# Spatial weights of the gating unit: loaded and masked between the halves of the v projection, transposed right behind the row statistics

## The chip, the cores and the metric

The kernel runs on one core of a Trainium2 chip, as one launch. The metric is the device time of one execution in microseconds (us); the time of a kernel is the median of its runs. Engines are named as in the profile: PE (TensorE matmul), PEld (its weight load), DVE (VectorE), ACT (ScalarE), POOL (GpSimd), SP (SyncE, which issues nearly all DMAs here).

## What is computed

Two blocks follow one another on a sequence of 1024 rows of width 1024, all in float32. The first block has two layers (`DEPTH = 2`), and only these are touched by the change. A layer normalizes and modulates its input, multiplies it with `w_in`, and splits the product into u, v, z_a (512 columns each) and the parts of a sparse attention (q, k, val, z_b, and an indexer q_idx, k_idx, w_idx that picks 256 keys for each row). The gating unit is

```
vn = layer_norm(v, g_v, b_v).reshape(bn, s // CHUNK, CHUNK, A_GROUPS, A_GDIM)
w_m = jnp.where(causal[None], w_s, jnp.zeros_like(w_s))
mixed = jnp.einsum('gts,bcsgd->bctgd', w_m, vn) + b_s.T[:, :, None]
return u * mixed.reshape(bn, s, A_WIDTH)
```

so `w_spatial` (8 groups of 128x128) must be masked to its lower triangle and stand on the chip transposed before it can multiply the normalized v. Then silu(z_a) times this, next to the gated attention, goes through `w_out`, and a layer norm ends the layer. The second block (windowed attention, convolution, a mixture of 32 experts) takes the other half of the time and is not changed.

## The kernel before

The 1024 rows are 8 tiles of 128 partitions. A float32 product is made of three matmuls on split operands (`mm3`, lines 100 to 102): hi x hi, hi x lo, lo x hi. `dense_nat` is one projection of 256 columns: 8 k-steps, 8 row tiles, three matmuls each, into two tiles of PSUM ("big"); it takes its weights from `wnext`, which loads 128x512 (`wraw`, L136), rounds it on ACT (`whi`, L108) and subtracts on POOL (`wlo`, L111). In a layer the projections come in the order narrow columns, q_idx (two halves, six tiles), v (two halves, evacuated into X[:, :, 0] by `ev_c`, L781), u (two halves, into X[:, :, 1]), q (two halves), z_a, z_b.

Work that isn't projection is spread among the matmuls in two ways. Generators in the list `bgs` are stepped by `bg`, which `dense_nat` calls 16 times with 650 units each (10,400 a projection; 487.5 and 7,800 where six tiles are projected); a generator yields the units that a step costs, and the list is worked off in order. `flush(bgs)` behind the u projection runs what is left. In `streams` run the two selections of keys (`select`, tiles 2, 4, 6 and 3, 5, 7): transposes of q_idx (`heads_T`, L538, evacuated to `qT` by L543 and L544), score matmuls (L628), relu on ACT into `rel` (L631), weighted sums on DVE (L634, L636), then a search of many short DVE instructions (L606 to L686).

In `bgs` stand first `ada_late` (three parts in layer 0, one in layer 1; a part has two halves, a half has four loads of `adaw`, eight DVE products of 650 units, L463 and L465, and three more steps, 8,300 units in all), then `sgu`, the gating unit. `sgu` loads the norm's rows `vg`, loads `ws` and masks it on POOL (L795), loads the bias `bs`, takes the statistics of eight tiles (L802, L803; 700 units each), makes `rsv` (L84) and `nbv` (L808), normalizes each tile on ACT (L811) and multiplies and adds `vg` on POOL (L812, L813; 1,400 units each), transposes `ws` by `to_T` (PE L504 into two PSUM banks "tr", ACT L506 into `wmh`, DVE L507 into `wml`; 1,300 units), and then for each of eight groups splits v into `vs` (ACT L108, POOL L111), multiplies by `wmh` and `wml` on PE and applies u and the bias on DVE (L830).

`adaw`, `vg`, `ws`, `wmh`, `wml` and `vs` share one ring of four buffers, the tag "w4"; the two banks "tr" also serve `heads_T`; `rel`, `code`, `pl` and the accumulators of `ada_late` share six buffers, the tag "r2". The kernel is first traced in the order of the Python code; a scheduler then gives each engine its own fixed order, by readiness in a model of time and, among ready instructions, by the order of tracing. So a load stands in SP's queue where its buffer came free, not where the code has it.

Of the kernel before, what the change touches and what calls it, by code (L numbers as in the profile page):

```python
# [26 lines left out]
NT = 8  # L27
# [13 lines left out]
def tile_hybrid(ctx, tc, I, out):  # L41
# [18 lines left out]
    def bank(shape, kind):  # L60
        if kind in banks["turn"]:
            n = banks["turn"][kind] % banks[kind]
            banks["turn"][kind] += 1
            if n < 2:
                return psum2.tile(shape, FT, name=kind)
            return banks["pool"].tile(shape, FT, name=kind + "x", bufs=banks[kind] - 2)
        return banks["pool"].tile(shape, FT, name=kind, bufs=banks[kind])
# [13 lines left out]
    def rsqrt(dst, var, eps, n):  # L81
        t = small.tile([128, 16], FT, name="rsq")
        V.tensor_scalar(t[:, :n], var, eps, None, op0=OP.add)
        G.tensor_tensor(dst, t[:, :n], mhalf[:, :n], op=OP.pow)  # L84
# [14 lines left out]
    def mm3(o, lh, ll, rh, rl, start, stop):  # L99
        T.matmul(o, lh, rh, start=start, stop=False, skip_group_check=True)  # L100
        T.matmul(o, lh, rl, start=False, stop=False, skip_group_check=True)  # L101
        T.matmul(o, ll, rh, start=False, stop=stop, skip_group_check=True)  # L102

    def split(hi, lo, src, which="pool", sub=None):
        if which == "pool":
            G.tensor_scalar(hi, src, 1.0, 0.0, op0=OP.mult, op1=OP.add)
        elif which == "act":
            A.activation(hi, src, AF.Copy)  # L108
        else:
            V.tensor_copy(hi, src)  # L110
        return (sub or V).tensor_tensor(lo, src, hi.bitcast(FT), op=OP.subtract)  # L111
# [37 lines left out]
    def wnext():  # L149
        if not ready:  # L150
            ready.append(wstage(*plan.pop(0)))
        r = ready.pop(0)
        if plan and plan[0] is None:
            plan.pop(0)
        elif plan:
            ready.append(wstage(*plan.pop(0)))
        return r
# [44 lines left out]
    def bg(budget, ns=None):  # L202
        due[0] += budget
        while bgs and due[0] > 0:
            due[0] -= step(bgs)
        if not bgs:
            due[0] = 0.0
        now[0] += budget * 2.0 if ns is None else ns
        while True:
            ready = [x for x in streams if not x[2] or now[0] >= x[1] + MARGIN]  # L210
            if not ready:
                break
            s_ = min(ready, key=lambda x: x[1])
            if max(dve[0], s_[1]) > now[0] + AH:
                break
            resume(s_)
# [10 lines left out]
    def dense_nat(n, KT, lhs, tiles, evac, bgt=1300.0):  # L227
        nb = (len(tiles) + 3) // 4
        ps = [bank([128, 4, 256], "big") for _ in range(nb)]
        for k0 in range(0, KT, 2):  # L230
            hi, lo = wnext()
            for b in range(nb):
                for kk in range(2):
                    k = k0 + kk
                    for i in range(4 * b, min(4 * b + 4, len(tiles))):
                        t = tiles[i]
                        mm3(ps[b][:, i % 4, :n], lhs(k, 0, t), lhs(k, 1, t), hi[:, kk, :n], lo[:, kk, :n],
                            start=(k == 0 and i % 2 == 0), stop=(k == KT - 1))
                    if k + 1 == KT:
                        for i in range(4 * b, min(4 * b + 4, len(tiles)), 2):  # L240
                            evac(tiles[i], ps[b][:, i % 4:i % 4 + 2, :n])
                    bg(bgt * len(tiles) / 8 / nb, 3 * min(4, len(tiles) - 4 * b) * n / 2.4)
# [35 lines left out]
    def load_row(dst, src, n):  # L278
        nc.sync.dma_start(dst, rows_of(src, n))
# [220 lines left out]
    def to_T(src, t, hi, lo, n, half=None):  # L500
        for b in range(n // 4) if half is None else (half,):
            ps = bank([128, 4, 128], "tr")
            for j in range(4):
                T.transpose(ps[:, j, :], src[:, (b * 4 + j) * 128:(b * 4 + j + 1) * 128], ident)  # L504
            d = (slice(None), slice(b * 4, b * 4 + 4), slice(t * 128, (t + 1) * 128))
            A.activation(hi[d], ps, AF.Copy)  # L506
            V.tensor_tensor(lo[d], ps, hi[d].bitcast(FT), op=OP.subtract)  # L507
# [51 lines left out]
    def layer(l, xin, hT=None):  # L559
# [4 lines left out]
        lhs = lambda k, a, t: hT[a][:, k, t * 128:(t + 1) * 128]  # L564
# [214 lines left out]
        def ev_c(sl, c, scale=1.0):  # L779
            def f(t, ps):  # L780
                A.activation(X[:, t:t + 2, sl, c * 256:(c + 1) * 256], ps, AF.Copy, scale=scale)  # L781
            return f
        for c in range(2):
            dense_nat(256, 8, lhs, range(NT), ev_c(0, c))

        def sgu():
            vg = tmp.tile([128, 2, 512], FT, name="vg", tag="w4", bufs=4)
            load_row(vg[:, 0, :], I["v_norm_g"][l], 512)
            load_row(vg[:, 1, :], I["v_norm_b"][l], 512)

            wmh = tmp.tile([128, 8, 128], FR, name="wmh", tag="w4", bufs=4)
            wml = tmp.tile([128, 8, 128], FR, name="wml", tag="w4", bufs=4)
            ws = tmp.tile([128, 8, 128], FT, name="ws", tag="w4", bufs=4)
            nc.sync.dma_start(ws, I["w_spatial"][l].rearrange("g t s -> t g s"))
            G.affine_select(ws, ws, pattern=[[0, 8], [-1, 128]], compare_op=OP.is_ge, fill=0.0, base=0,  # L795
                            channel_multiplier=1)
            bs = small1.tile([128, 8], FT, name="bs", bufs=1)
            nc.sync.dma_start(bs, I["b_spatial"][l].rearrange("g t -> t g"), allow_slow_non_contiguous=True)
            mvs = small1.tile([128, NT, 2], FT, name="mvs", bufs=1)
            for t in range(NT):  # L800
                st = small1.tile([128, 6], FT, name="bst1")
                V.bn_stats(st, X[:, t, 0, :])  # L802
                V.bn_aggr(mvs[:, t, :], st)  # L803
                yield 700.0, 650.0
            rsv = small1.tile([128, NT], FT, name="rsv", bufs=1)
            rsqrt(rsv, mvs[:, :, 1], 1e-5, NT)
            nbv = small1.tile([128, NT], FT, name="nbv", bufs=1)
            V.scalar_tensor_tensor(nbv, mvs[:, :, 0], -1.0, rsv, op0=OP.mult, op1=OP.mult)  # L808
            for t in range(NT):
                xv = X[:, t, 0, :]  # L810
                A.activation(xv, xv, AF.Identity, scale=rsv[:, t:t + 1], bias=nbv[:, t:t + 1])  # L811
                G.tensor_tensor(xv, xv, vg[:, 0, :], op=OP.mult)  # L812
                G.tensor_tensor(xv, xv, vg[:, 1, :], op=OP.add)  # L813
                yield SG1
            to_T(ws.rearrange("p g s -> p (g s)"), 0, wmh, wml, 8)
            yield 1300.0, 1200.0
            vss = {}
            for g in range(9):
                if g < 8:
                    vs = vss[g] = tmp.tile([128, 2, NT, 64], FR, name="vs", tag="w4", bufs=4)  # L820
                    split(vs[:, 0], vs[:, 1], X[:, :, 0, g * 64:(g + 1) * 64], "act", G)
                    yield SG2
                if g == 0:
                    continue
                g -= 1
                vs = vss.pop(g)
                ps = bank([128, NT, 64], "sm")
                mm3(ps, wmh[:, g, :], wml[:, g, :], vs[:, 0], vs[:, 1], True, True)
                xu = X[:, :, 1, g * 64:(g + 1) * 64]
                V.scalar_tensor_tensor(xu, ps, bs[:, g:g + 1], xu, op0=OP.add, op1=OP.mult)  # L830
                yield SG3, 660.0
# [298 lines left out]
    lhs = lambda k, a, t: hT[a][:, k, t * 128:(t + 1) * 128]  # L1130
# [486 lines left out]
    def gather(tcol, b):  # L1617
        return G.indirect_dma_start(out=XG[b][0:SL], out_offset=None, in_=h2d,
                             in_offset=bass.IndirectOffsetOnAxis(ap=tcol, axis=0), bounds_check=S - 1, oob_is_err=False)

    def split_e(raw):
        w_ = mo.tile([128, 2, 8 * 256], FR, name="ew", bufs=3)
        for h in range(2):
            c = slice(h * 1024, (h + 1) * 1024)
            split(w_[:, 0, c], w_[:, 1, c], raw[:, c], "act", V)
        return w_
# [55 lines left out]
    for e in range(NXG - 1):  # L1682
        g = gather(ti[:, e:e + 1], e)
# [3 lines left out]
    xTs, hid, ws, wds = {0: prep(0)}, {}, {}, {}  # L1687
# [47 lines left out]
    with tc.For_i(0, nov, 1) as b:  # L1735
# [14 lines left out]
        ws = [split_e(r) for r in raw]  # L1750
# [38 lines left out]
```

## Time and profile before

| | |
|---|---|
| median of 3 runs | 2372.64 us (2372.11 to 2374.22) |
| the profiled execution | 2371.94 us, span of the trace 2369.8 us |
| PE busy, PEld busy | 2140.5 us (90%), 1883.9 us (79%) |
| DVE, ACT, POOL busy | 1521.2, 1082.8, 1082.0 us |
| layer 0, layer 1, second block begin at about | 60, 700, 1310 us |

The profile is one execution. Its own time is 2.1 us above the span and 0.7 us under the median. A wait of an engine is named by what released it. The granted TensorE clock is a share of 2.4 GHz.

### The profile page before, as it was taken

The numbers are of one execution on the slowest core, as the hardware profiler recorded it, in microseconds if no ns is written. First come the engines' busy times: TensorE is split into PE (matmuls) and PEld (weight loads), VectorE is DVE, ScalarE is ACT, GpSimd is POOL, SyncE is SP. The second block draws the span as 40 slices with busy tenths as digits, with TensorE's granted clock in tenths as the row PEclk, the third lists the DMA queues.
The fourth block names the chain that finished last, engine by engine and source line by source line (L and its number), as shares of the span: only waits on it lengthen the run. The fifth ranks groups of instructions, "written<-read, shape, count | busy, mean of one in ns | idle before, by whom it ended". The sixth has DMA issues, their size and how long they took to land. (4 is left out here: it accounts for less than half of the span.)

```text
span 2369.8 us, 35974 instructions
## 1 busy us (share of the span) xinstructions
PE 2140.5 (90%) x13235; PEld 1883.9 (79%) x13235; DVE 1521.2 (64%) x3191; ACT 1082.8 (46%) x1943; POOL 1082.0 (46%) x1018
## 2 busy tenths in 40 slices
PE   5998998798989979997998999999999797999896
PEld 4898897587879979876887888888888586888785
DVE  9768887677753769685776348861010345888784
ACT  4333443554642443436554335652121222778774
POOL 4664575556736553845554345532244412222221
PEclk9999998899999989998999999999999998999998
DMA  7522112312114111223111111122121256999994
GB/s 239 188 79 86 53 32 81 106 59 68 41 47 138 45 36 49 66 67 108 68 45 41 44 41 34 30 52 67 49 67 45 98 209 200 311 325 326 317 329 116
DMA packets 146392, 260.88 MB, mean 110 GB/s; under 512 B 24681, under 2 KB 101889, under 8 KB 133905
## 3 DMA queue, kind: packets, MB, share of 16 engines
q1 hardware_dynamic: 139024, 241.59, 31.1%
q0 software_dynamic: 7168, 16.79, 3.2%
q8 instruction: 105, 1.72, 0.3%
q14 instruction: 95, 0.77, 0.1%
HBM read 228.83 MB, written 37.90 MB: 113 GB/s over the span
## 5 line engine op out<-in xcount | busy, mean ns | idle before, releaser
L111 POOL TENSOR_TENSOR wlo<-wraw,whi 128x512 fp32r<-128x512 f32 (+1 forms) x188 | 249.8, 1329 | 484.9 <-ACT whi L108 459.2
L101 PE MATMUL big<-wlo,s 128*128 128x256 f32 (+1 forms) x1536 | 440.4, 288 | 16.0 <-POOL wlo L111 16.0
L100 PE MATMUL big<-whi,s 128*128 128x256 f32 (+1 forms) x1536 | 437.8, 289 | 13.6 <-ACT s L506 8.4
L102 PE MATMUL big<-whi,s 128*128 128x256 f32 (+1 forms) x1536 | 439.6, 288 | 0.0
L101 PEld LDWEIGHTS big<-wlo,s 128*128 128x128 f32 x1536 | 301.2, 196 | 22.8 <-POOL wlo L111 19.6
L100 PEld LDWEIGHTS big<-whi,s 128*128 128x128 f32 x1536 | 298.6, 196 | 21.9 <-ACT s L506 11.0
L102 PEld LDWEIGHTS big<-whi,s 128*128 128x128 f32 x1536 | 300.6, 196 | 3.1 <-issue 0.9
L108 ACT ACTIVATE whi<-wraw 128x512 fp32r<-128x512 f32 (+1 forms) x188 | 117.7, 627 | 385.2 <-PE big L102 127.2
L111 DVE TENSOR_TENSOR ew<-s,ew 128x1024 fp32r<-128x1024 f32 x138 | 162.8, 1220 | 39.0 <-ACT ew L108 37.9
L636 DVE SCALAR_TENSOR_TENSOR s<-rel,widx,s 128x384 f32<-128x384 f32 (+3 forms) x140 | 130.6, 957 | 85.1 <-ACT rel L631 83.6
L100 PE MATMUL sm<-ew,xT 128*96 128x256 f32 x512 | 147.6, 288 | 4.8 <-ACT xT L1636 4.8
L108 ACT ACTIVATE ew<-s 128x1024 fp32r<-128x1024 f32 x138 | 137.7, 1050 | 28.6 <-PE sm L102 18.8
L102 PE MATMUL sm<-ew,xT 128*96 128x256 f32 x512 | 148.6, 290 | 1.3 <-DVE xT L1637 1.2
L101 PE MATMUL sm<-ew,xT 128*96 128x256 f32 x512 | 146.3, 286 | 0.9 <-DVE ew L111 0.9
L631 ACT ACTIVATE rel<-sm 128x384 f32<-128x384 f32 (+3 forms) x160 | 80.5, 522 | 124.1 <-PE sm L628 114.7
L100 PE MATMUL half<-s,whi 128*128 128x512 f32 x320 | 130.7, 408 | 7.1 <-ACT s L953 3.1
L101 PE MATMUL half<-s,whi 128*128 128x512 f32 x320 | 128.7, 402 | 0.0
L102 PE MATMUL half<-s,wlo 128*128 128x512 f32 x320 | 127.3, 401 | 0.0
L1674 POOL DMA_INDIRECT out_dram<-yt,ti x32 | 58.2, 1820 | 136.0 <-DMA out_dram<-yt,ti 61.0
L606 DVE TENSOR_SCALAR_CACHE_REDUCE bias<-code,cand 128x512 bf16<-128x512 int16 (+5 forms) x126 | 114.1, 924 | 0.5
L878 POOL TENSOR_SCALAR Z<-Z,rc 128x128 f32<-128x128 f32 (+7 forms) x88 | 63.9, 738 | 83.3 <-DVE rc L876 50.7
L100 PE MATMUL big<-s,whi 128*128 128x512 f32 x256 | 99.7, 390 | 0.3 <-DVE convf L1335 0.3
(618 smaller groups left out, 6014.3 us busy)
## 6 DMA issues: line engine op xcount, KB each, us to landing
wraw<-in_w_in_dram SPq DMA_DIRECT2D x164, 256.0 KB, 2.8
adaw<-in_w_ada_dram SPq DMA_DIRECT2D x48, 512.0 KB, 4.5
s<-in_w_gate_e_dram SPq DMA_DIRECT2D x23, 1024.0 KB, 9.2
s<-in_w_up_e_dram SPq DMA_DIRECT2D x23, 1024.0 KB, 11.0
s<-in_w_down_e_dram SPq DMA_DIRECT2D x23, 1024.0 KB, 11.3
X<-in_w_gate_e_dram SPq DMA_DIRECT2D x9, 1024.0 KB, 10.1
X<-in_w_up_e_dram SPq DMA_DIRECT2D x9, 1024.0 KB, 9.8
X<-in_w_down_e_dram SPq DMA_DIRECT2D x9, 1024.0 KB
```

Source lines behind the costliest of these rows:

```text
L100: T.matmul(o, lh, rh, start=start, stop=False, skip_group_check=True)
L101: T.matmul(o, lh, rl, start=False, stop=False, skip_group_check=True)
L102: T.matmul(o, ll, rh, start=False, stop=stop, skip_group_check=True)
L108: A.activation(hi, src, AF.Copy)
L111: return (sub or V).tensor_tensor(lo, src, hi.bitcast(FT), op=OP.subtract)
L606: V.tensor_scalar(junk[:, :src.shape[1]], src, thr, 0.0, op0=op, op1=OP.add, accum_out=cnt)
L631: A.activation(rel[:, :w_], ps[:, :w_], AF.Relu, scale=0.125)
L636: V.scalar_tensor_tensor(d, rel[:, :w_], widx[:, i, h:h + 1], d, op0=OP.mult, op1=OP.add)
L878: G.tensor_scalar(P[hh][:, :n], P[hh][:, :n], rc[:, hh:hh + 1], 1.0, op0=OP.mult, op1=OP.mult)
L1674: return G.indirect_dma_start(out=out, out_offset=bass.IndirectOffsetOnAxis(ap=ycol, axis=0), in_=yt, in_offset=None, bounds_check=S - 1, ...
```

## The change

The loads of `vg`, `ws` and `bs` and the mask of `ws` move out of `sgu` into a function `sgu_in`, which is called once between the two halves of the v projection instead of behind them, so it is traced ahead of those steps of `ada_late` that are still to come. The transposes of `ws` with their evacuations (`to_T`) move from behind the eight normalizations to a place between `rsv` and `nbv`. No instruction is added or removed, and no unit of `bg` changes.

```
-        for c in range(2):
-            dense_nat(256, 8, lhs, range(NT), ev_c(0, c))
-
-        def sgu():
+        def sgu_in():
             vg = tmp.tile([128, 2, 512], FT, name="vg", tag="w4", bufs=4)
...
+            return vg, ws, wmh, wml, bs
+
+        gin = []
+        for c in range(2):
+            if c:
+                gin.append(sgu_in())
+            dense_nat(256, 8, lhs, range(NT), ev_c(0, c))
+
+        def sgu():
+            vg, ws, wmh, wml, bs = gin[0]
             mvs = small1.tile([128, NT, 2], FT, name="mvs", bufs=1)
...
             rsqrt(rsv, mvs[:, :, 1], 1e-5, NT)
+            to_T(ws.rearrange("p g s -> p (g s)"), 0, wmh, wml, 8)
+            yield 1300.0, 1200.0
             nbv = small1.tile([128, NT], FT, name="nbv", bufs=1)
...
                 yield SG1
-            to_T(ws.rearrange("p g s -> p (g s)"), 0, wmh, wml, 8)
-            yield 1300.0, 1200.0
             vss = {}
```

## Rows read from the trace of the kernel before

**Rows 1.** The page: busy time and its share of the span, and busy tenths in 40 slices.

```profile
PE 2140.5 (90%) x13235; PEld 1883.9 (79%) x13235; DVE 1521.2 (64%) x3191; ACT 1082.8 (46%) x1943; POOL 1082.0 (46%) x1018
...
PE   5998998798989979997998999999999797999896
```

**Rows 2.** Waits of PE, first those of 60 to 700 us, then those of 700 to 1280 us: who waited for whom, us in total, times, longest.

```profile
PE tr L504 <- POOL ws L795: 4.0, 1, 4.0
...
PE tr L538 <- DVE wml L507: 9.0, 1, 9.0
```

**Rows 3.** The timeline of layer 0 about that wait, PE: start, us, instruction, and in brackets the idle time before it and its releaser.

```profile
230.28 0.39 PE L100 MATMUL big<-whi,s 128*128 128x256 f32 x1 [0.98 <-ACT X L781]
234.69 0.47 PE L504 MATMUL tr<-ident,ws 128*128 128x128 f32 x1 [4.02 <-POOL ws L795]
```

**Rows 4.** The timeline of POOL in layer 0.

```profile
220.55 11.24 POOL L812 TENSOR_TENSOR X<-X,vg 128x512 f32<-128x512 f32 x8 [3.83 <-DMA vg<-in_v_norm_g_dram]
231.75 1.58 POOL L813 TENSOR_TENSOR X<-X,vg 128x512 f32<-128x512 f32 x1
233.28 1.35 POOL L795 TENSOR_SCALAR_AFFINE_SELECT ws<-ws 128x1024 f32<-128x1024 f32 x1
```

**Rows 5.** The timeline of SP's queue, in layer 0 and then in layer 1.

```profile
105.43 2.88 SPq L458 DMA_DIRECT2D adaw<-in_w_ada_dram  x2
...
164.38 3.04 SPq L458 DMA_DIRECT2D adaw<-in_w_ada_dram  x2
...
215.60 0.35 SPq L279 DMA_DIRECT2D vg<-in_v_norm_g_dram  x1
...
217.30 0.38 SPq L794 DMA_DIRECT2D ws<-in_w_spatial_dram  x1
...
731.72 0.34 SPq L279 DMA_DIRECT2D vg<-in_v_norm_g_dram  x1
...
733.75 0.83 SPq L794 DMA_DIRECT2D ws<-in_w_spatial_dram  x1
```

**Rows 6.** Busy time in stretches: the stretch and its length, then PE, PEld, DVE, ACT, POOL (instructions), the granted clock, DMA share, GB/s.

```profile
230.70:234.70 4.00, 0.01 (x1) 0.01 (x1) 2.98 (x2) 0.24 (x1) 4.00 (x4) 0.94 0.00 0
234.70:239.60 4.90, 4.90 (x26) 4.71 (x27) 2.97 (x4) 2.94 (x6) 4.90 (x4) 0.70 0.04 5
...
186.00:214.00 28.00, 24.98 (x184) 24.48 (x183) 27.84 (x95) 10.12 (x16) 5.37 (x5) 0.88 0.28 77
...
810.00:830.00 20.00, 20.00 (x168) 20.00 (x167) 19.71 (x77) 8.77 (x15) 7.75 (x6) 1.00 0.13 34
830.00:850.00 20.00, 7.02 (x31) 5.22 (x30) 19.97 (x45) 5.67 (x11) 20.00 (x16) 0.71 0.17 52
850.00:855.20 5.20, 5.20 (x24) 5.20 (x24) 5.13 (x12) 1.39 (x3) 1.21 (x1) 0.50 0.00 0
```

**Rows 7.** The timeline of layer 1, PE.

```profile
841.41 2.26 PE L538 MATMUL tr<-ident,Z 128*128 128x128 f32 x8 [8.97 <-DVE wml L507]
843.32 2.82 PE L628 MATMUL sm<-kist,qT 128*128 128x384 f32 x8
849.32 0.90 PE L628 MATMUL sm<-kist,qT 128*128 128x320 f32 x2 [3.18 <-ACT rel L631]
850.02 0.41 PE L101 MATMUL big<-wlo,s 128*128 128x256 f32 x1
```

**Rows 8.** The timeline of layer 1: two lines of DVE's own listing and one of ACT's, then two of POOL's.

```profile
841.82 0.67 DVE L507 TENSOR_TENSOR wml<-tr,wmh 128x512 fp32r<-128x512 f32 x1
...
847.51 1.22 DVE L634 TENSOR_SCALAR s<-rel,widx 128x384 f32<-128x384 f32 x1
...
848.83 0.44 ACT L631 ACTIVATE rel<-sm 128x320 f32<-128x320 f32 x1 [3.36 <-DVE s L634]
...
834.40 5.68 POOL L812 TENSOR_TENSOR X<-X,vg 128x512 f32<-128x512 f32 x4
...
841.71 2.49 POOL L111 TENSOR_TENSOR wlo<-wraw,whi 128x512 fp32r<-128x512 f32 x2
```

**Rows 9.** DVE by line and shape: count, busy us, mean ns of one. First two of 186 to 212 us (layer 0), then the same two and one more of 834 to 850 us (layer 1).

```profile
L683 DVE SCALAR_TENSOR_TENSOR bias<-s,lcand,bias 128x512 bf16<-128x512 f32 x1 | 0.7, 745 | 0.0
...
L670 DVE SCALAR_TENSOR_TENSOR s<-bias,s 128x384 f32<-128x384 bf16 x1 | 0.6, 550 | 0.0
...
L683 DVE SCALAR_TENSOR_TENSOR bias<-s,lcand,bias 128x512 bf16<-128x512 f32 x1 | 1.7, 1746 | 0.0
L670 DVE SCALAR_TENSOR_TENSOR s<-bias,s 128x384 f32<-128x384 bf16 x1 | 1.6, 1624 | 0.0
...
L606 DVE TENSOR_SCALAR_CACHE_REDUCE bias<-code,cand 128x384 bf16<-128x384 int16 x1 | 0.6, 589 | 0.0
```

**Rows 10.** The instructions on the tile `adaw` in 60 to 240 us: how long DVE sat idle for its loads (us, times), and a load's time to landing.

```profile
  DMA adaw<-in_w_ada_dram: 0.3, 1
...
DMA to landing us min/median/max: 3.9/4.4/5.2
```

**Rows 11.** The waits of PE for the split groups of v in layer 0 (timeline of PE).

```profile
275.58 0.51 PE L100 MATMUL sm<-vs,wmh 128*128 128x512 f32 x1 [1.44 <-ACT vs L108]
276.94 0.50 PE L101 MATMUL sm<-vs,wmh 128*128 128x512 f32 x1 [0.85 <-POOL vs L111]
278.44 0.67 PE L101 MATMUL sm<-vs,wmh 128*128 128x512 f32 x1 [0.55 <-POOL vs L111]
```

## The prediction

> **What bounds the kernel now.** The page comes first: PE is busy for 90% of the span and below eight tenths in 7 of its 40 slices [rows 1]. PE's order is fixed, so what can be won is a stretch in which PE stands still, and each must be read where it lies. The waits of PE by releaser, over the two layers, name the two that the change is about: 4.0 us in layer 0 for the mask of `ws`, and 9.0 us in layer 1 for `wml`, the low half of the transposed weights [rows 2]. The timelines say what stands behind each.
>
> Layer 0: PE has done its work at 230.7 and begins the transposes at 234.69 [rows 3]. It waited for POOL, and POOL was late by its queue: the mask stood behind eight multiplications with `vg` and one addition, and the first of these had itself waited until 220.55 for the load of `vg` [rows 4]. SP shows why: `vg` and `ws` were issued at 215.60 and 217.30, after the last `adaw`, because the w4 buffers were held by `adaw` until then [rows 5]. POOL had little to do before, 5.37 of 28 us in 186 to 214 [rows 6], so all of this is a matter of buffers.
>
> Layer 1: there `vg` and `ws` were issued at 731.72 and 733.75, a hundred us ahead of their use [rows 5]. What made PE wait was a bank "tr": `wml` was written late by DVE, at 841.82 for the second half, and only then the transposes of q_idx could start, at 841.41 for the first bank [rows 7, 8]. But DVE was busy for 19.71 and 19.97 of 20 us in the stretches around it [rows 6]; it was late with everything.
>
> **The change, part by part.** The terms are taken against the profiled execution, 2371.94 us, which is 0.7 under the median of 2372.64; the 0.7 is put back at the end.
>
> *Loads and mask in layer 0.* When `sgu_in` is traced, the list has worked off 7,800 + 7,800 + 10,400 = 26,000 units, three halves of `ada_late` (24,900) and two products of the fourth, so 13 of 24 `adaw` are ahead of `vg` and `ws` and 11 behind. The sixteenth `adaw` was issued by 108 us, the seventeenth at 164 [rows 5]. I expect `vg` and `ws` to take the places of the fourteenth to sixteenth, at some 100 to 110 us, at the latest those of 164 to 173. The mask is one instruction of 1.35 us on POOL [rows 4], then long over when the transposes come. So the 4.02 us of waiting [rows 3] go. After it PE ran for 4.90 us at a granted clock of 0.70 [rows 6], part of it on the lower level of 1.2 GHz; at full clock that work is 0.70 x 4.90 = 3.4 us, so 1.5 go too. Sum: -5.5 us.
>
> What is late next there? DVE was waiting itself in that stretch (busy 2.98 of 4.00), ACT too (0.24) [rows 6]. POOL was not: 4.00 of 4.00, and it would be the next bound if the multiplications stayed where they are. They don't: with `vg` on the chip they can follow the normalizations directly and lie in the 28 us in which POOL had 22.6 free. Sixteen of them at 11.24 / 8 = 1.4 us [rows 4] are 22.5 us, which just fits. So the early `vg` is the half that matters.
>
> *The 11 loads of `adaw` that now come behind.* `vg`, `wmh` and `wml` hold three of the four buffers until the additions are done, so a half of `ada_late` loads its four tiles through one or two buffers and each load of 4.4 us [rows 10] may show on DVE. Before, DVE idled for these loads once, 0.3 us [rows 10]. Below, the bound is nothing, for nobody near waits for the modulation rows; above I take 0.3 for each of the eleven, 3.3 us (all eleven in full, 48 us, would need DVE to have nothing else to do between them). I take nothing, because DVE had 2.98 of 4.00 where the first half of them would end up. On SP the later `adaw` may stand ahead of a `wraw`, whose buffers are three; covered as long as one split is ready ahead.
>
> *The mask on POOL at 100 to 120 us* adds 1.35 us there and takes it away later; 0 to +1.35, taken 0. The load of `bs` does not depend on its place in the code. In layer 1 the list had only 16,600 units of `ada_late`, so `vg`, `ws` and the mask stay where they were: 0.
>
> *The transposes ahead of `nbv`.* The eight transposes, two evacuations on ACT and two on DVE are the same instructions at the same price, 11,200 units earlier. ACT takes `wmh` ahead of the eight normalizations, which come later by two evacuations; behind them stand POOL's multiplications, not PE. In layer 1 the bank is then free when PE wants it, and the 8.97 us go from that place. What is late next is DVE: PE's next wait, 3.18 us at 849.32, is for `rel`, which ACT could write only after DVE's L634 at 847.51 had taken an older one [rows 7, 8]. In front of that L634 DVE had at most 0.3 us of gaps in 37 us [rows 6], and moving `wml` forward within a full queue does not shorten it. The transposes and scores that PE did from 841.41 to 846 would be done earlier and PE would then stand until the same 849. So layer 1 is taken at 0, with bounds from 0 to -(8.97 + 3.18) and another 0.50 x 5.2 = 2.6 of lower clock (granted clock 0.50 in the 5.2 us behind) [rows 6], -14.8.
>
> *The split groups of v in layer 0* (1.44 + 0.85 + 0.55 = 2.8 us) [rows 11] wait through a pair of `vs` buffers, which stay a pair; the earlier additions let the first pair start earlier, not the third group. Taken 0, bound -2.8.
>
> Sum: 2371.94 - 5.5 = 2366.4, with 0.7 **2367.1**. Its own range runs from 2364.3 (rows 11 too) to 2371.8 (mask and `adaw` at their upper bounds, +4.7).
>
> **The rivals.** *Layer 1's wait goes as well.* The order on the engines is made anew, and if the scores' L634 come ahead of the search's tail on DVE, or big matmuls ahead of the scores on PE, the whole -14.8 is won: 2352.3. For it: the wait is booked on exactly the bank that the change frees. Against it: DVE full at 19.97 of 20.
>
> *Nothing is won.* `vg` and `ws` get no buffer before 210 us because `adaw` keep all four, or the wait of 4 us moves to a `wlo` that now stands behind a multiplication on POOL. Then 2372.6. For the second: in layer 1 two `wlo` came at 841.71, behind 5.68 us of multiplications and one addition [rows 8]. Against the first: the trace order puts `vg` and `ws` ahead of eleven loads.
>
> *Slower: layer 0 becomes like layer 1.* With `vg` early, POOL's 22.5 us of multiplications move from beside the scores into 187 to 212 us, beside the search's tail of tiles 2 and 3, which in layer 0 was undisturbed. In layer 1 they already lie so, and there the two-input instructions of the tail are long: L683 1746 ns for 745, L670 1624 for 550, while the one-input count L606 stays at 589 [rows 9]. Eight such instructions (L670, L679, L683, L685 for two tiles) at about +1.0 make DVE 8 us later in a stretch in which it had 27.84 of 28 us [rows 6], and the first scores of tiles 4 and 5 queue behind it. If this costs PE in layer 0 all that the same neighbourhood goes with in layer 1, 8.97 + 3.18 + 2.6 = 14.8 us, the net is +9.3: 2381.9. It is slower by what can be told from the point at which PE loses more than 5.5 + 4.7 = 10.2 us. Against it: in layer 0 the scores begin at 218, some 30 us behind the first multiplication instead of 7, and products of `ada_late`, now held back by buffers, leave DVE room just there. The Trainium skill (SBUF — State Buffer, section "Who interferes with whom") states the mechanism as a rule: a DVE instruction with two SBUF inputs and a GpSimd instruction that reads SBUF share a port pair, and one that comes second waits for the whole other instruction. The trace agrees by the pairs above, 745 to 1746 ns beside 1.4 us multiplications; the rule speaks against this move, which the two waits of PE alone would not tell.
>
> **How the numbers follow.** A measurement of this kernel can tell about 0.2%, 4.7 us, from no change: 2367.9 and 2377.4 are the borders. Forecast 0.45, of which 0.30 under 2367.9 and 0.15 above; layer 1 too 0.13; nothing 0.15; slower 0.27. So faster 0.43, same 0.30, slower 0.27. The range reaches to the rivals on both sides, which are single prices with a spread of their own, 2352 to 2382: about half of each rival's outcomes at the ends, 2 in 10 together, lie outside.
>
> **What would show it.** Right: `vg` and `ws` issued ahead of 175 us in layer 0, multiplications of POOL from about 188, no wait of PE for `ws`, POOL with room from 220 on; in layer 1 the transposes at some 825 us, PE still standing before 849 with `rel` as releaser and DVE full. Wrong: a wait of PE for `wlo` or `rel` in 190 to 235 us of layer 0 (the slower rival, with L683 and L670 of layer 0 above 1.5 us); a stretch 830 to 850 with PE well above 7.02 us (the first rival); or loads still at 215. The forecast also fails where the new order moves waits in q, z_a or the attention behind, which no row here prices: they are made from the same queues by another order.

## The result, and the profile after

The changed kernel takes 2390.94 us (median of 4 runs, 2385.96 to 2394.9) against 2372.38 us of the kernel before beside it (4 runs): a ratio of 1.0073, 95% interval 1.0055 to 1.0092, some 18.5 us slower. The profiled execution, the fastest of the four, took 2385.96 us with a span of 2384.0, 14.2 more than that of before. Lines of code below the edit have new numbers: the mask is L792, the normalizations L820, the multiplications and additions with `vg` L821 and L822, the attention's lines 7 higher.

PE is as busy as before, and its dips lie elsewhere: the fourth slice (179 to 238 us) is now a 6, to be held against [rows 1].

```profile
PE 2140.5 (90%) x13235; PEld 1880.6 (79%) x13235; DVE 1521.5 (64%) x3191; ACT 1085.2 (46%) x1943; POOL 1074.0 (45%) x1018
...
PE   5996998798989979987999899999999797999996
```

The loads are where they were expected, ahead of eleven `adaw`, of which the last come at 216 us and later (SP's queue, layer 0; compare [rows 5]).

```profile
102.25 0.35 SPq L279 DMA_DIRECT2D vg<-in_v_norm_g_dram  x1
...
104.74 0.38 SPq L791 DMA_DIRECT2D ws<-in_w_spatial_dram  x1
107.26 0.37 SPq L458 DMA_DIRECT2D adaw<-in_w_ada_dram  x1
...
164.34 3.04 SPq L458 DMA_DIRECT2D adaw<-in_w_ada_dram  x2
...
191.51 0.37 SPq L458 DMA_DIRECT2D adaw<-in_w_ada_dram  x1
...
215.97 0.39 SPq L458 DMA_DIRECT2D adaw<-in_w_ada_dram  x1
...
217.56 4.91 SPq L458 DMA_DIRECT2D adaw<-in_w_ada_dram  x4
```

POOL's timeline in layer 0 shows what the early `vg` released. Eleven multiplications and additions stand ahead of the first `wlo`.

```profile
187.98 2.56 POOL L821 TENSOR_TENSOR X<-X,vg 128x512 f32<-128x512 f32 x2 [1.87 <-ACT X L820]
...
195.41 5.38 POOL L821 TENSOR_TENSOR X<-X,vg 128x512 f32<-128x512 f32 x4
200.74 1.71 POOL L822 TENSOR_TENSOR X<-X,vg 128x512 f32<-128x512 f32 x1
202.41 3.26 POOL L111 TENSOR_TENSOR wlo<-wraw,whi 128x512 fp32r<-128x512 f32 x2
205.63 7.05 POOL L822 TENSOR_TENSOR X<-X,vg 128x512 f32<-128x512 f32 x5
```

On PE the wait for the mask [rows 3] is gone: four of the transposes run at 172 us and four at 190.88, without one (the mask was made at 111 us). Two larger waits stand in its place, one for that `wlo`, one for a product of `ada_late`.

```profile
190.88 0.60 PE L504 MATMUL tr<-ident,ws 128*128 128x128 f32 x4
...
204.18 0.58 PE L101 MATMUL big<-wlo,s 128*128 128x256 f32 x1 [10.26 <-POOL wlo L111]
...
221.61 1.87 PE L469 MATMUL sm<-ada,onesf 128*1 128x512 f32 x2 [8.52 <-DVE ada L465]
```

DVE by line in 195 to 221 us (count, busy us, mean ns of one, idle time before) answers to [rows 9]; most pairs here are one instruction of 512 columns and one of 384. L670 and L683, two-input instructions of the search's tail, are now as long in layer 0 as in layer 1. `L695` works on 8 columns and takes 973 ns in the mean: the first three of the four run beside POOL's work with `vg`, 1.13 us the first and 2.47 for the next two together, and the fourth, behind POOL's last addition, takes 0.21.

```profile
L465 DVE SCALAR_TENSOR_TENSOR ada<-adaw,cb,ada 128x512 f32<-128x512 f32 x7 | 5.2, 745 | 0.5 <-DMA adaw<-in_w_ada_dram 0.5
L695 DVE SCALAR_TENSOR_TENSOR e<-rank,K,m 128x8 f32<-128x8 f32 x4 | 3.8, 973 | 0.0
L670 DVE SCALAR_TENSOR_TENSOR s<-bias,s 128x512 f32<-128x512 bf16 (+1 forms) x2 | 3.4, 1684 | 0.0
L683 DVE SCALAR_TENSOR_TENSOR bias<-s,lcand,bias 128x512 bf16<-128x512 f32 (+1 forms) x2 | 3.4, 1680 | 0.0
L679 DVE SCALAR_TENSOR_TENSOR pl<-s,lcand,place 128x512 f16<-128x512 f32 (+1 forms) x2 | 2.4, 1206 | 0.0
...
L606 DVE TENSOR_SCALAR_CACHE_REDUCE bias<-code,cand 128x384 bf16<-128x384 int16 (+1 forms) x3 | 2.0, 653 | 0.0
L463 DVE TENSOR_SCALAR ada<-adaw,cb 128x512 f32<-128x512 f32 x1 | 1.5, 1515 | 0.0
```

In layer 1 the two waits of [rows 7] are still there, 11.9 us for 12.2: what is saved on `wml` is waited for `rel`.

```profile
853.62 2.17 PE L538 MATMUL tr<-ident,Z 128*128 128x128 f32 x8 [5.79 <-DVE wml L507]
...
864.74 0.90 PE L628 MATMUL sm<-kist,qT 128*128 128x320 f32 x2 [6.07 <-ACT rel L631]
```

**Where the time went.** To place a loss, each ACT and DVE instruction of one trace is matched with the same one of before (same text of the line, same tiles, the n-th of its kind), and the median of the differences in start is taken over a stretch. The table gives the delay added (+) or made up (-) in each stretch in us, the stretches in the time of before: up to 185; from there to 515 (layer 0's gating, scores, projections); to 700 (layer 0's attention and output); to 1000 (layer 1 up to its attention); to 1160 (layer 1's attention); to 2190 (the rest). Behind 2190 us the changed kernel makes up 3.5 again, which gives the 14.2 of the spans. An entry moves by up to 1.5 us with the place at which a stretch is cut. The runs below the first are the experiments.

```
run                start  to 515  to 700  to 1000  to 1160  to 2190   sum
changed kernel      -0.1    +5.3    +9.2     +0.7     +4.0     -1.4  17.7
e1_loads_only       +0.1    +5.5    +9.6     +0.1     +0.8     +1.6  17.7
e2_transposes_only  +3.5    +0.7     0.0     -2.4    +11.8     +0.3  13.9
e3_vg_late          +1.2    -6.5    +4.4     -2.5    +15.1     -2.7   9.0
e4_layer1_only      +3.7    -2.3    -0.1     -2.8    +12.8     -3.1   8.2
n1_short_mults      -0.1   -12.8    +8.0     -0.6     +6.4     +2.7   3.6
e5_ws_layer0        +0.5    -5.8    +4.3     -1.1     +6.3     -0.6   3.6
c1_stats_number     -0.4    -2.5    -0.4     +0.3     +6.9     -1.0   2.9
c2_rope_number      +2.6    -2.4    +7.6     +0.5     +4.5     +1.2  14.0
v1_ws0_z1250        +3.3    -4.5    +1.4     -1.1     +2.6     -1.3   0.4
v2_layer1_s1000     +2.3    +1.1    +0.1     +0.9     +1.7     +3.2   9.3
v3_both_late_vg     -0.1    -2.6    +1.9     +1.0     +1.0     +1.6   2.8
v4_after_r3500      +0.3    +2.5     0.0     -0.1     +8.0     -1.8   8.9
q1_wlo_ahead        +2.4    +3.6    +8.1     +0.5     +6.1     +0.9  21.6
```

Single executions differ by themselves. Four runs have layer 0 in the order of before (e2, e4, c1, v2): they lie between -0.4 and +3.7 us in the first column and between -2.5 and +1.1 in the second. v2 is built in the order of before on every engine from start to end, as far as the traces tell, and its row is the plainest measure of this spread: its traced execution, 2379.89 us, is 9.3 behind, its median of 2374.71 is level with before. The traced execution of c1 is the fastest of its eight (2372.18 for a median of 2379.94). So a row shows where time went; what a kernel costs is told by its median. The attentions repeat better: in the third column the five runs that draw layer 0's attention in the order of before (those four and v4) stay within 0.4, and runs with one and the same other order agree (changed kernel and e1: 9.2 and 9.6; e3 and e5: 4.4 and 4.3). The changed kernel loses 5.3 ahead of layer 0's attention, 9.2 in it, and 4.0 in layer 1's: more than half of the loss of this execution lies in stretches whose code the change doesn't touch.

### The profile page after: what moved, and what is told of

The parts are those of the page before. It is cut to its first block, busy times and chain, and to the rows that moved or that the text cites. A ratio compares the mean times of both kernels' runs of the same rounds, so it can differ in the third digit from the quotient of the medians.

```text
span 2384.0 us, 35978 instructions
## 1 busy us (share of the span) xinstructions
PE 2140.5 (90%) x13235; PEld 1880.6 (79%) x13235; DVE 1521.5 (64%) x3191; ACT 1085.2 (46%) x1943; POOL 1074.0 (45%) x1018
## 5 line engine op out<-in xcount | busy, mean ns | idle before, releaser
L636 DVE SCALAR_TENSOR_TENSOR s<-rel,widx,s 128x384 f32<-128x384 f32 (+3 forms) x140 | 121.6, 891 | 87.9 <-ACT rel L631 86.4
L606 DVE TENSOR_SCALAR_CACHE_REDUCE bias<-code,cand 128x512 bf16<-128x512 int16 (+5 forms) x126 | 113.7, 924 | 0.3
L1681 POOL DMA_INDIRECT out_dram<-yt,ti x32 | 50.1, 1565 | 133.7 <-DMA out_dram<-yt,ti 76.0
```

Source lines behind the costliest of these rows:

```text
L606: V.tensor_scalar(junk[:, :src.shape[1]], src, thr, 0.0, op0=op, op1=OP.add, accum_out=cnt)
L636: V.scalar_tensor_tensor(d, rel[:, :w_], widx[:, i, h:h + 1], d, op0=OP.mult, op1=OP.add)
L1681: return G.indirect_dma_start(out=out, out_offset=bass.IndirectOffsetOnAxis(ap=ycol, axis=0), in_=yt, in_offset=None, bounds_check=S - 1, ...
```

## The experiments

The theories were: A, the multiplications with `vg`, done early, are the direct loss; B, the earlier transposes are; C, the build makes the order of the engines anew for any edit, and an attention drawn anew costs by itself; D, `adaw` is starved of buffers; E, a gain ahead of an attention turns into waits in it. Each run stands with its median, that of the kernel before beside it, and the ratio with its 95% interval.

**e1_loads_only.** The changed kernel with the transposes put back:

```
-            to_T(ws.rearrange("p g s -> p (g s)"), 0, wmh, wml, 8)
-            yield 1300.0, 1200.0
             nbv = small1.tile([128, NT], FT, name="nbv", bufs=1)
...
                 yield SG1
+            to_T(ws.rearrange("p g s -> p (g s)"), 0, wmh, wml, 8)
+            yield 1300.0, 1200.0
```

> The changed kernel with its transposes put back behind the normalizations: the loads and the mask stay early, in both layers. Theory A (the early load of vg releases POOL's sixteen multiplications and additions into the search's tail of layer 0; the big matmul's wlo stands behind them, 10.3 us, and DVE's two-input instructions lengthen): the whole loss stays, 2386 to 2394, with a wait of PE for wlo of about 10 us at 194 to 204 us. Theory B (the transposes ahead of nbv are what costs, for ACT's and DVE's evacuations come ahead of the normalizations): 2367 to 2373, without that wait. Theory C (any redrawn order of the later stages can lose ten us): no fixed time, but the first 220 us like the changed kernel's and another loss behind them than its 8 us.

Measured: 2388.45 beside 2375.0, ratio 1.0048 (1.0036 to 1.006), in the range of A. The wait for `wlo` is 10.3 us again, and the table's row is that of the changed kernel up to 1000 us, within 0.6. Layer 0's loss is that of the loads alone; B falls for layer 0. Layer 0 of both kernels has one and the same order on every engine: moving the transposes in the code moved nothing there. Layer 1 of e1 is in the order of before, and its attention loses 0.8.

**e2_transposes_only.** The kernel before with those two lines moved ahead of `nbv`, the loads where they were.

> The kernel before with the transposes alone moved ahead of nbv: vg, ws and the mask are still issued at some 215 us in layer 0. Theory A: no multiplication of POOL comes early, so no loss by wlo; PE stands for the load of ws instead of the mask, since the transposes come earlier on PE than the load lands (about 222): a wait of 4 to 10 us, so 2372 to 2380, and layer 1 within 3 us of before. Theory B: the loss of the change, 2385 to 2394, with layer 1 taking part in it.

Measured: 2384.28 beside 2375.0, ratio 1.0034 (1.0023 to 1.0046), above the range of A and just under that of B. Layer 0 is in the order of before (the wait for the mask is 4.6 us instead of 4.0). In layer 1 PE waits 5.7 us for `wml` and 6.5 at most for `rel`, as in the changed kernel, and right behind these waits, at 852 to 870 us, the delay is what it was at 780 to 820 (4.8 us for 4.9). Then the row makes up some 3 us between 870 and 970 us and loses 11.8 in the attention. So the earlier transposes don't cost where they stand, as B had it; something behind them does.

**e3_vg_late.** The changed kernel with the three lines of `vg` back at the head of `sgu`:

```
-            vg = tmp.tile([128, 2, 512], FT, name="vg", tag="w4", bufs=4)
-            load_row(vg[:, 0, :], I["v_norm_g"][l], 512)
-            load_row(vg[:, 1, :], I["v_norm_b"][l], 512)
...
         def sgu():
-            vg, ws, wmh, wml, bs = gin[0]
+            vg = tmp.tile([128, 2, 512], FT, name="vg", tag="w4", bufs=4)
+            load_row(vg[:, 0, :], I["v_norm_g"][l], 512)
+            load_row(vg[:, 1, :], I["v_norm_b"][l], 512)
+            ws, wmh, wml, bs = gin[0]
```

> The changed kernel with vg alone loaded at its old place, behind the first half of the next projection; ws, the mask and the transposes stay early. Theory A: POOL's multiplications of layer 0 stay behind 205 us where they were, the wait for wlo (10.3 us) and the long tail of DVE go, the wait for the mask stays away: 2366 to 2373. Theory D (the adaw loads behind wmh and wml come just in time and the matmul of ada_late waits 8.5 us for them): the wait at L469 stays at 5 us or more and the time at 2380 or above. Theory B: 2385 to 2394.

Measured: 2383.72 beside 2375.0, ratio 1.0038 (1.0025 to 1.0051). The direct part is as A says: the longest wait for `wlo` is 3.8 us, L670 and L683 are back at 616 and 680 ns, L469 waits no more for `ada` (against D, but `vg` leaves its buffer to `adaw` too here), and between 185 and 515 us the kernel gains 6.5 us on before. Then 4.4 and 15.1 us go in the two attentions. A has the right place and the wrong total (2366 to 2373 was expected).

**e4_layer1_only.** `gin` is filled, and the transposes are early, only where `l` is 1.

> The change in layer 1 alone; layer 0 is as before. The prediction's step (DVE is full there, moving wml within a full queue shortens nothing) says 0: 2370 to 2375, with the layer's end within 2 us of before. The rival that was given 0.13 (the waits of 8.97 and 3.18 us and the slow clock behind go): 2357 to 2363. Theory B: layer 1 has a loss of its own, 2376 or above.

Measured: 2380.54 beside 2375.0, ratio 1.0026 (1.0015 to 1.0037). The time lies in B's range, and B is not the reason: the order is that of e2 on every engine, and of e3 in layer 1. Behind the two waits, at 852 to 870 us, the delay has changed by 0.2 us, up to 1000 us the row makes up 2.8, and in the attention 12.8 are lost. The windows and the waits of PE over that stretch (972 to 1110 us) show PE standing for `Z` and `pt`, the attention's own steps (before's longest waits for them are 3.7 and 1.3 us):

```profile
972.00:1110.00 138.00, 107.97 (x590) 93.22 (x588) 89.85 (x222) 60.23 (x132) 83.90 (x91) 0.86 0.26 84
```

```profile
PE trx L902 <- POOL Z L889: 5.5, 1, 5.5
PE tr L902 <- POOL Z L889: 5.5, 2, 4.6
...
PE sm L917 <- DVE pt L911: 4.2, 1, 4.2
```

All four runs lose 9 us or more in an attention that no edit touches. The next four ask whether that is the order alone.

**n1_short_mults.** The changed kernel with

```
+                w = 512 if l else 16
+                G.tensor_tensor(xv[:, :w], xv[:, :w], vg[:, 0, :w], op=OP.mult)
+                G.tensor_tensor(xv[:, :w], xv[:, :w], vg[:, 1, :w], op=OP.add)
```

> The changed kernel whose sixteen POOL instructions with vg in layer 0 work on 16 of 512 columns (496 columns of v_norm_g and v_norm_b are left out of the result there). The loads, buffers and the place of everything stay. Theory A (POOL's queue and the long DVE instructions are the direct loss): the 10.3 us wait for wlo is under 1 us, L670 and L683 of layer 0 are back at 0.6 to 0.7 us, and the kernel is level with before or ahead (0 to 4 us) at 300 us. Theory D (adaw starved of buffers): the wait at L469 stays at 5 us or more. For the rest: if the order of layer 0's attention costs by itself (theory C), the loss of some 10 us at 525 to 620 us is still there and the time is 2378 to 2386; if that loss was the consequence of being late before, it goes, and the time is 2368 to 2374.

This kernel leaves out the multiplication and the addition for 496 of 512 columns in layer 0. Measured: 2375.46 beside 2373.21, ratio 1.0012 (0.9999 to 1.0026), between the two expected ranges. At 290 to 335 us the kernel is 9.6 us ahead of before, more than the 0 to 4 expected, where the changed one was 7.3 behind: where it now lies, the work with `vg` costs 16.9 us against a kernel that hardly does it (before does it in full, only later). Waits of PE, 180 to 320 us:

```profile
PE big L101 <- POOL wlo L111: 1.4, 2, 0.8
...
PE sm L469 <- DVE ada L465: 0.6, 1, 0.6
```

L683 is back at 680 ns and L670 at 822. D can't be told from A by this run, because `vg` gives its buffer back sooner and `adaw` come sooner too. The changed kernel's own trace tells it: up to the product L469 DVE stood idle 0.5 us for `adaw` (the first line of DVE above), of the 8.5 us that PE waited. Layer 0's attention still loses 8.0 us and layer 1's 6.4, although this kernel comes to both ahead of time.

**e5_ws_layer0.** Weights and mask early in layer 0 alone, `vg` and the transposes as before (`if c and not l: gin.append(sgu_in())`).

> Only the weights and their mask come early, only in layer 0; vg and the transposes stay, and layer 1's code is that of before. The program that is built has layer 0 in the same order as the kernel with vg late, and layer 1 in an order of its own, though nothing in its code differs from before. Theory A: layer 0 gains, 2 to 5 us ahead of before at 225 to 550 us. Without theory C layer 1 adds nothing: 2368 to 2373. By theory C layer 1, redrawn, adds between -5 and +15 by its stretches from 1000 us on: 2367 to 2388.

Measured: 2378.18 beside 2373.21, ratio 1.0022 (1.0009 to 1.0035). Layer 0 gains 5.8 us from 185 to 515 us; the attentions take 4.3 and 6.3, the second in a layer whose code is that of before.

**c1_stats_number** and **c2_rope_number**, the controls, each one number of the kernel before:

```
-                yield 700.0, 650.0
+                yield 1000.0, 650.0
```

```
-                yield 3000.0
+                yield 4000.0
```

> A control: the kernel before with one number of the list changed (the statistics of v yield 1000 instead of 700), nothing of the change in it. The program that is built has layer 0 in the same order on PE, and layer 1 redrawn from the spatial gating on and through its attention. Theory C: a gain or loss of several us, up to 15, that arises in layer 1 from 830 us on, half of it or more in the attention (1000 to 1110 us). If orders drawn anew cost nothing by themselves: 2371 to 2377.

> A second control: the kernel before with another number changed (a rotation of q yields 4000 instead of 3000). Layer 0 is as before up to its attention, which is redrawn, as parts of layer 1's and of the last layer are. Theory C: a gain or loss of several us, up to 15, in layer 0's attention (450 to 640 us), the stretch in which the changed kernel loses 10. Otherwise 2371 to 2377.

Measured: 2379.94 and 2379.37 beside 2373.21, ratios 1.0038 (1.0024 to 1.0052) and 1.0037 (1.0022 to 1.0051). Nothing of the change is in them, and both are slower than before by 6 to 7 us. c1's traced execution loses 6.9 us in layer 1's attention, c2's 7.6 in layer 0's and 4.5 in layer 1's. Waits of PE over layer 0's attention (505 to 655 us) of the changed kernel, then (500 to 648) of c2: the same instructions wait, four of these five by the same amounts. The third list is before (500 to 640), where `pth`, `s` and `ptl` cost 0.6, 0.6 and 0.5 us.

```profile
PE sm L911 <- ACT pth L906: 4.1, 2, 3.5
PE sm L913 <- DVE ptl L907: 3.2, 4, 1.6
PE half L100 <- DVE s L1052: 2.9, 1, 2.9
PE tr L898 <- POOL Z L885: 1.4, 1, 1.4
PE sc L875 <- DVE mx L876: 1.3, 2, 0.9
```

```profile
PE sm L904 <- ACT pth L899: 4.1, 2, 3.5
PE half L100 <- DVE s L1045: 2.9, 1, 2.9
PE sm L906 <- DVE ptl L900: 1.8, 3, 0.7
PE tr L891 <- POOL Z L878: 1.4, 1, 1.4
PE sc L868 <- DVE mx L869: 1.3, 2, 0.9
```

```profile
PE sc L868 <- DVE mx L869: 2.1, 2, 1.7
...
PE half L100 <- DVE s L1045: 0.6, 1, 0.6
PE sm L904 <- ACT pth L899: 0.6, 2, 0.4
PE sm L906 <- DVE ptl L900: 0.5, 2, 0.3
```

By the traces c2 runs layer 0's attention in the very order of the changed kernel on every engine, and so do e1 and q1 below. By the table c2 comes to it 0.2 us behind before and loses 7.6 in it, the changed kernel comes 5.2 behind and loses 9.2; e2, in the order of before, comes 4.2 behind and loses nothing. So those waits come with the order, and neither with the change's own lines nor with the delay ahead of them. The next four kernels were picked the other way round: by one or two numbers for which the built program has the attentions near the order of before.

**v1_ws0_z1250** is e5 with `ZBB` (the units that a call in the z_b projection gives the list) at 1250 instead of 1300; **v2_layer1_s1000** is e4 with c1's number; **v3_both_late_vg** is e3 with `ZBB` 1250 and `SG1` (the units of a normalization's step) at 1200 instead of 1400; **v4_after_r3500** is the changed kernel with c2's number at 3500.

> The weights and their mask early in layer 0 alone (vg and the transposes where they were), with one number of the list beside it (ZBB 1250 instead of 1300), chosen because the program that is built then has PE's order in both attentions close to that of before (263 rows of layer 0's attention stand elsewhere instead of 498, 68 of layer 1's instead of 1656). Theory C (what the earlier runs lost in the attentions is the price of an order drawn anew): some 5 us ahead of before at 475 us, at most 2 us given back in layer 0's attention, at most 1 in layer 1's; 4 to 7 us below before. Theory E (a gain ahead of an attention turns into waits inside it, whatever the order, since DVE's search sets its pace): the 5 us are gone at 650 us; within 2 us of before.

> The change in layer 1 alone, with the statistics' number at 1000 instead of 700, chosen because the built program then has layer 1's attention nearly in the order of before (62 rows elsewhere instead of 645). Theory C: layer 1 is some 4 us ahead at 975 us, as in the run of the change in layer 1 alone, and keeps it through the attention, in which that run lost 12: 2 to 5 us below before. Theory E, and the prediction's step that DVE is full there: the 4 us are given back in the attention; within 2 us of before. If the loss of that run came from the earlier transposes themselves: 6 to 10 us above before.

> The two parts that gained ahead of the attentions together: weights and mask early, transposes early, vg late, with two numbers (ZBB 1250, SG1 1200) for which both attentions are drawn close to before (263 and 100 rows elsewhere). Theory C: both gains are kept, 5 in layer 0 and 4 in layer 1, less some 2: 5 to 9 us below before. Theory E: within 2 us of before.

> The changed kernel with one number (a rotation of q yields 3500 instead of 3000), for which layer 0's attention stands nearer to before's order (317 rows elsewhere instead of 582). The multiplications with vg, the wait for wlo and the starved adaw stay. Theory C: the 5 us of delay at 475 us stay, and of the 10 us in layer 0's attention 3 to 10 go: 8 to 16 us above before. If those 10 us follow from the delay ahead of it: 16 to 20 us above before.

Measured beside 2374.06: v1 2371.58, ratio 0.9992 (0.9979 to 1.0005); v2 2374.71, 1.0005 (0.999 to 1.0021); v3 2373.05, 0.9993 (0.9979 to 1.0007); v4 2381.99, 1.0037 (1.0023 to 1.0051). The times of the first three miss what C had forecast: v1 is 2.5 us below before (C: 4 to 7, E: within 2), v2 0.7 above and v3 1.0 below (C: 2 to 5 and 5 to 9 below, E: within 2). v4, 7.9 above, lies at the lower edge of C's 8 to 16. In v4 the 9.2 us of layer 0's attention are gone wholly, with the 2.5 us of delay ahead of it still there. Busy time over that stretch (columns as in [rows 6]) of before, the changed kernel and v4:

```profile
500.00:640.00 140.00, 130.94 (x751) 110.76 (x750) 107.09 (x273) 79.52 (x138) 102.82 (x75) 1.00 0.17 54
```

```profile
505.00:655.00 150.00, 135.60 (x753) 114.26 (x751) 112.17 (x273) 80.53 (x140) 103.35 (x75) 0.97 0.15 50
```

```profile
503.00:643.00 140.00, 130.96 (x750) 110.87 (x749) 106.84 (x273) 79.58 (x139) 103.08 (x75) 1.00 0.17 54
```

The same matmuls take 140 us in v4 and in before and 150 in the changed kernel, of which 4.7 are PE's own time at a granted clock of 0.97. v2 and v3 lose 1.7 and 1.0 in layer 1's attention where e4 and e3 lost 12.8 and 15.1. So C holds for what it says of the attentions. That a gain ahead is kept through them is not shown, and E is not excluded: v1 gains 4.5 from 185 to 515 us and gives back 1.4 and 2.6, v3 gives back 1.9 of its 2.6, and v2 has the order of before throughout, so it has the change in its code and not in its program and tests no gain. No version is faster than before by what can be told.

**q1_wlo_ahead** parts the queue of POOL from the long instructions of DVE:

```
-        split(hi[:, :, :c], lo[:, :, :c], raw[:, :, :c], "act", G)
+        lows.append(split(hi[:, :, :c], lo[:, :, :c], raw[:, :, :c], "act", G))
...
-                G.tensor_tensor(xv, xv, vg[:, 0, :], op=OP.mult)
+                m = G.tensor_tensor(xv, xv, vg[:, 0, :], op=OP.mult)
+                if l == 0:
+                    follow(m, lows[(-5, -5, -5, -4, -4, -4, -3, -3)[t]].ins.name, "behind the split")
```

> The changed kernel in which, in layer 0, the multiplications with vg are ordered behind those splits whose wlo PE needs next: POOL does two wlo first, then six multiplications and additions, a wlo, four, a wlo, and so on, all at full length. If the queue is the loss: the wait for wlo falls from 10.3 us to 3 us or less, and at 300 us the kernel is level with before or up to 4 us ahead, where the changed kernel was 7 behind. If DVE's long instructions are the loss: L670 and L683 stay at 1.5 us or more, and at 300 us the kernel is still 5 to 9 us behind. If both: 0 to 5 behind, with a wait at L469 of 5 us or more. The attentions are drawn anew (theory C) and may add up to 15, so the whole time is no test: 2372 to 2392.

Measured: 2389.19 beside 2373.45, ratio 1.0065 (1.0043 to 1.0087). Waits of PE, 180 to 320 us:

```profile
PE sm L470 <- DVE ada L466: 13.3, 1, 13.3
...
PE big L101 <- POOL wlo L111: 0.9, 1, 0.9
```

DVE by line, 187 to 230 us:

```profile
L466 DVE SCALAR_TENSOR_TENSOR ada<-adaw,cb,ada 128x512 f32<-128x512 f32 x7 | 8.6, 1228 | 0.1
...
L684 DVE SCALAR_TENSOR_TENSOR bias<-s,lcand,bias 128x512 bf16<-128x512 f32 (+1 forms) x2 | 3.4, 1711 | 0.0
```

The wait for `wlo` is gone and the loss is not: less what it had lost before 185 us, the kernel is 8.7 - 2.4 = 6.3 us behind at 290 to 335, the changed one 7.4. PE waits 13.3 us for `ada` instead of 8.5. The queue of POOL was the first of two gates in a row; behind it DVE, full from 190 to 220 us (10.0 of 10 in each ten, and 9.9 of the next), sets the time. Of the two long instructions named beforehand L683 (here L684) stayed above 1.5 us, L670 (here L671) is at 1363 ns: its 384 columns at 1.58 us, its 512 at 1.14.

## Why the prediction was wrong

The forecast was 2367.1, with a range of 2352 to 2382; the time is 2390.94, outside the range and on the other side.

**Loads and mask, right.** `vg` and `ws` were issued at 102 and 105 us, ahead of eleven `adaw`; the mask was long done; the 4.0 us went. e3, e5, v1 and v3, which keep only this part of layer 0, gain 6.5, 5.8, 4.5 and 2.6 us from 185 to 515 us, 4.9 in the mean, where the four runs with layer 0 in the order of before gain 0.8 in the mean by chance. So this part is worth about 4 us, an estimate from a few executions; the -5.5 was right in sign and perhaps a little large.

**The step that failed first** is that the sixteen multiplications and additions are "22.5 us, which just fits. So the early `vg` is the half that matters". POOL's free 22.6 us were counted, and not what is done beside them on DVE and behind them on POOL; the sum had no term for it. e3 keeps the gain without the early `vg`, and against e3 the changed kernel loses 11.8 us from 185 to 515 us (+5.3 for -6.5); against n1, which hardly does the work at all, it loses 16.9. The slower rival had the mechanism, and with 14.8 a price between these two. Its signs came as they stood under "Wrong": a wait for `wlo` at 194 to 204 us, with L683 and L670 at 1680 and 1684 ns. What was held against it was partly misread: the row of 834.40 [rows 8] isn't the first of layer 1's multiplications.

```profile
826.49 2.56 POOL L812 TENSOR_TENSOR X<-X,vg 128x512 f32<-128x512 f32 x2 [1.99 <-ACT X L811]
```

So layer 1's scores follow the first multiplication by some 17 us (843.32), not by 7, and layer 0 was less unlike it than the prediction took it to be.

The Trainium skill (SBUF — State Buffer, section "Who interferes with whom") states the rule of that rival: a DVE instruction with two SBUF inputs and a GpSimd instruction that reads SBUF contend, and the one that comes second is blocked for the whole of the other. The trace agrees: the 8 columns of L695 take 973 ns in the mean instead of 216, while L606, with one tensor, stays at 653 (674 before).

The `wlo` behind a multiplication, named under "nothing is won", was also there; q1 shows that it isn't the only gate.

**With it failed** "nobody near waits for the modulation rows". PE does: the product L469 has its place in PE's fixed order, and the scores stand behind it. The `adaw` were bounded at 3.3 us by DVE's idle time; DVE's idle time for them is 3.2 us (2.3 + 0.9 in 186 to 245 us), within the bound, and only 0.5 of it lies ahead of the product; the price is PE's wait, 8.5, and 13.3 in q1. So at most 0.5 of the 8.5 is loads that came late. For the rest DVE was busy, with its long instructions and with its fixed order of search and products; these two weren't parted.

**Layer 1 at 0, right in its mechanism.** PE waits less for `wml` (5.8 us instead of 9.0) and more for `rel` (6.1 instead of 3.2), 11.9 in all instead of 12.2, as the step had it that DVE is full and the wait would move. e2 and e4 show the same two waits and no gain behind them. What these two make up later, between 870 and 970 us, comes with another order there; e3, in that order too, does the same.

**The largest term had no place in the sum.** The last sentence of the prediction says that q, z_a and the attention behind are made "by another order" that no row prices. The controls price it: attentions drawn anew cost 4.3 to 9.6 us in layer 0 (seven runs with three orders) and 4.0 to 15.1 in layer 1 (ten runs with six, where orders that differ in two or three instructions count as one), with or without the change, and -0.4 to +2.6 where they were drawn as before or near to it. In the changed kernel this is 9.2 + 4.0 of the 17.7. So even the slower rival, whose net was +9.3, missed the time. No draw was better than that of before. That before has a favourable order is what the runs show; which of its instructions stand better was not settled.

## What to carry to other kernels

Free time of an engine is not free for any work: see what reads the same memory beside it, what stands behind it in its own queue, and which product in PE's fixed order waits for the engine that it slows; when one gate is removed, the next may take most of it back (with the 10.3 us for `wlo` gone, the wait for `ada` grew from 8.5 to 13.3). Where a build makes the whole order anew, run a control that changes a number and no work: here it moved the time by 6 to 7 us, more than the wait of 4 us that the change was about. And place a loss by stretches before explaining it; a median alone would have put all 18.5 us on the edit's own lines. Check as well that the built order differs from before at all: v2 had the edit in its code and the old order in its program.

## What was not expected of the hardware

A DVE instruction of 8 columns with two inputs grew from 216 to 973 ns in the mean beside POOL's 1.3 us multiplications, more in proportion than those of 384 and 512 columns (L683: 676 to 1680). L463, with one tensor as input and float32 on both sides, is long beside POOL too: 1515 ns, where n1 has 484. Before has both lengths, 1.52 us at 203.90 beside a `wlo` of POOL (203.56 to 205.13) and 0.47 at 211.38 with POOL idle. And in layer 0's attention the changed kernel's PE stood idle for 14.4 of 150 us where before had 9.1 of 140, and the granted clock was 0.94 in three stretches of 30 us, part of each on the lower level of 1.2 GHz, where before and v4 have 1.00 throughout; the same matmuls took 4.7 us longer.
